# Two-block network on one core: the inverse's rank-1 updates on GpSimd instead of VectorE, a shorter round trip through DRAM sent by SyncE, and retention's table loaded with the other constants

## The chip, the cores and the metric

The kernel runs on one core of a Trainium2 chip. The metric is the device time of one execution in microseconds. A core has TensorE (PE, matrix products), VectorE (DVE), ScalarE (ACT), GpSimd (POOL) and SyncE (SP, which here only issues DMAs). Each engine works through its own list of instructions in the order of the program; an instruction that waits holds up everything behind it on its engine. The order is set when the kernel is built, by a scheduler that places instructions by priority and by its own estimate of when their inputs will be there; nothing is reordered while the kernel runs.

## The reference, cut to what matters

Two blocks of two layers each work on 256 tokens of width 1,024. Only the first block's two layers are touched. Each has a mixer with two branches, a gated delta rule and a retention:

```
lhs = jnp.eye(CHUNK) + a_mat                       # unit lower triangular
u = triangular_solve(lhs, vc * bc, ...)
w = triangular_solve(lhs, kb * exp(gc), ...)
...                                                # scan over chunks gives o
y_gdn  = (norm(o) * silu(gz)) @ w_br_gdn
scores = einsum(qc, kc) * dmask                    # retention, dmask = powers of a decay
y_ret  = (norm(retention) * silu(rg)) @ w_br_ret
merged = sigmoid(mg_ret) * y_ret + sigmoid(mg_gdn) * y_gdn
h = h + merged @ w_out
```

All weights and products are float32.

## The kernel before, in words

Every weight product is done in split float32: a block of weights (`raw`, 512 KB, six buffers, loaded by SP at L168) is copied by ACT to a rounded high part (`whi`, L247) and subtracted by DVE for the low part (`wlo`, L248), and TensorE then runs three matmuls (L195 to L197, or L221 to L223 for the transposed form) for each pair of tiles. One `raw` feeds 12 matmuls of 512 columns. There are three buffers of the pair `whi`, `wlo`. So the chain raw, whi, wlo, matmul runs all through the kernel, and the mixer's other work is put between its links.

In the mixer (`mixer1`, once per layer) `keys` makes the matrices `A` (8 heads by 2 chunks of 128, so 16 triangles of 128x128). Their inverses are needed by the delta rule. `small_blocks` inverts the 64 diagonal blocks of 32x32 of these 16 triangles: it sends the blocks of `A` through DRAM (`da`, L480, L486), so that one partition holds one block and half of its columns (`X`, named `na` in the code), starts from the unit matrix (`t`, tile `X2`), and applies 31 rank-1 updates, each a multiply into `w32` (L491) and a subtraction (L493). A transposed copy (`tt`, L494) is made, and both `t` and `tt` go back through DRAM (`dt`, L498, L499) into `tc32` (L501; shown as `tc` in the profile), with the blocks across partitions again. All these DMAs are issued by ACT. `invert` then builds `Tt` (L531) and `Tn` (L539) from `tc32` and joins the 32x32 blocks into 128x128 inverses, by small matmuls (L549 to L569) with a copy on ACT or a subtraction on DVE between each and the next; it is called for heads 0 to 3 (`i0`) and 4 to 7 (`i1`). `delta` (`d0`, `d1`) applies the delta rule to them (L585 to L633). `ORDER` names the sequence in which these and the gate and rotary projections are written; the scheduler interleaves them.

After that the retention runs in a pool of its own: two transposes per head (L696), a copy (`qkt`, L699, on ACT), scores (L701, L702), a multiplication by the table `ret` (`st`, L704, on DVE), and the output (L707 to L709), with the gates `mgg` and `mgr` (L640) between. The table is loaded in that pool (L690), whose memory becomes free when the delta rule's pool is done with it.

Of the kernel before, what the change touches and what calls it, by code (L numbers as in the profile page):

```python
# [9 lines left out]
F32 = mybir.dt.float32  # L10
# [5 lines left out]
P = 128  # L16
# [5 lines left out]
RAW2 = 6  # L22
CONV = 800
CRIT = 50
DQ = lambda nc: [nc.scalar]
ORDER = "z v0 v1 v2 v3 rg i0 d0+i1 d1 rq rk rv".split()
D = 1024
T = 256
# [50 lines left out]
    return {k: np.ascontiguousarray(v, dtype=f) for k, v in out.items()}  # L79


C1 = ("ident", "tri", "mask32", "eye32", "cos", "sin")
C2 = ("cum", "band", "bmask", "chunk")
CONST_W = {"ident": 128, "cos": 256, "sin": 256, "ret": 1536, "incl": 128, "tri": 256, "mask32": 128, "eye32": 512, "cum": 512,
           "band": 1536, "bmask": 256, "chunk": 2, "lt8": 64, "iota": 128}
# [20 lines left out]
class Net:  # L106
# [246 lines left out]
    def mixer1(s, h, l):  # L353
        nc, a = s.nc, s.a
# [3 lines left out]
        with ExitStack() as es:  # L358
            g1 = es.enter_context(s.tc.tile_pool(name="g1", bufs=1))
# [23 lines left out]
            g = g1.tile([P, 2, 8], F32, name="g")  # L383
# [5 lines left out]
            tri = s.c["tri"].rearrange("p (i d) -> p i d", i=2)  # L389
# [28 lines left out]
            ga = gc = None  # L418
# [48 lines left out]
            Am = A.rearrange("p h c d -> p (h c) d")  # L467
            tc32 = None

            def small_blocks():  # L470


                nonlocal tc32
                tc32 = gc.tile([P, 16, 2, 32], F32, name="tc32", bufs=1)
                da = s.dram.tile([4, 16, 32, 32], F32, name="da")
                dt = s.dram.tile([32, 4, 16, 2, 32], F32, name="dt")
                q = DQ(nc)
                for b in range(4):
                    r = slice(b * 32, b * 32 + 32)
                    q[b % len(q)].dma_start(da[b].rearrange("m j i -> j m i"), Am[r, :, r])  # L480
                na = gc.tile([P, 8, P], F32, name="X", bufs=1).rearrange("p a (b c) -> p (a b) c", c=32)
                t = gc.tile([P, 8, 64], F32, name="X2", bufs=1).rearrange("p a (b c) -> p (a b) c", c=16)
                tt = gc.tile([P, 16, 32], F32, name="tt", bufs=1)
                w = gc.tile([P, 144], F32, name="w32", bufs=1)
                for e in range(2):
                    q[0].dma_start(na[e * 64:e * 64 + 64], da.rearrange("b m j i -> (b m) j i"))  # L486
                nc.vector.tensor_copy(t, s.c["eye32"].rearrange("p (a b) -> p a b", a=32))
                for j in range(31):
                    n, m = 31 - j, j // 2 + 1
                    x = w[:, :n * m].rearrange("p (a b) -> p a b", a=n)  # L490
                    nc.vector.tensor_mul(x, na[:, j, j + 1:][:, :, None].to_broadcast([P, n, m]),  # L491
                                         t[:, j, :m][:, None, :].to_broadcast([P, n, m]))
                    nc.vector.tensor_sub(t[:, j + 1:, :m], t[:, j + 1:, :m], x)  # L493
                nc.vector.tensor_copy(tt, t.rearrange("p a b -> p b a"))  # L494

                for e in range(2):
                    at = slice(e * 64, e * 64 + 64)
                    q[0].dma_start(dt.rearrange("r b m i (e c) -> e i (b m) r c", e=2)[e, 0], t[at])  # L498
                    q[0].dma_start(dt.rearrange("(r e) b m i c -> e i (b m) r c", e=2)[e, 1], tt[at])  # L499
                for b in range(4):  # L500
                    q[0].dma_start(tc32[b * 32:b * 32 + 32].rearrange("p m i c -> p (m i c)"),  # L501
                                   dt[:, b].rearrange("r m i c -> r (m i c)"))

            vts = {}

# [17 lines left out]
            def invert(pr):  # L523

                Tt = gc.tile([P, 8, P], F32, name="Tt")
                Tn = gc.tile([P, 8, P], F32, name="Tn", bufs=1)
                X2 = gc.tile([P, 8, 64], F32, name="X2", bufs=1)
                inverse[pr] = Tt
                Av = Am[:, pr * 8:pr * 8 + 8]
                own = slice(pr * 8, pr * 8 + 8)  # L530
                nc.vector.tensor_mul(  # L531
                    Tt.rearrange("p a (b c) -> p a b c", b=4),
                    tc32[:, own, 1][:, :, None, :].to_broadcast([P, 8, 4, 32]),
                    s.c["mask32"].rearrange("p (b c) -> p b c", b=4)[:, None].to_broadcast([P, 8, 4, 32]))
                nc.gpsimd.memset(Tn[:32, :, 32:64], 0.0)

                for b in range(3):
                    r = slice(b * 32, b * 32 + 32)
                    nc.vector.tensor_copy(Tn[r, :, r].rearrange("p a (c e) -> p a e c", e=2),  # L539
                                          tc32[r, own, 0].rearrange("p a (e c) -> p a e c", e=2))  # L540
                yield

                blocks = [(slice(b, b + 32), slice(b + 32, b + 64)) for b in (0, 64)]
                at = lambda i: slice(i * 32, i * 32 + 32)
                eight = lambda x: x[:, :T].rearrange("p (a d) -> p a d", a=8)
                px = s.pb()
                for l, r in blocks:
                    for i in range(8):
                        nc.tensor.matmul(px[r, at(i)], Av[l, i, r], Tn[l, i, l], start=True, stop=True)  # L549
                    nc.scalar.activation(X2[r, :, :32], eight(px[r]), AF.Copy)  # L550
                py = s.pb()
                l, r = blocks[0]
                for i in range(8):
                    nc.tensor.matmul(py[r, at(i)], Tt[r, i, r], X2[r, i, :32], start=True, stop=True)
                nc.scalar.activation(Tn[r, :, l], eight(py[r]), AF.Copy, scale=-1.0)
                pt = s.pb()
                for l, r in blocks:
                    for i in range(8):
                        nc.tensor.matmul(pt[l, at(i)], X2[r, i, :32], Tt[r, i, r], start=True, stop=True)
                    nc.vector.tensor_sub(Tt[l, :, r], Tt[l, :, r], eight(pt[l]))  # L560
                yield

                px = s.pb()
                for i in range(8):
                    nc.tensor.matmul(px[64:, i * 64:(i + 1) * 64], Av[:64, i, 64:], Tn[:64, i, :64], start=True, stop=True)
                nc.scalar.activation(X2[64:].rearrange("p a d -> p (a d)"), px[64:], AF.Copy)
                pt = s.pb()
                for i in range(8):
                    nc.tensor.matmul(pt[:64, i * 64:(i + 1) * 64], X2[64:, i], Tt[64:, i, 64:], start=True, stop=True)  # L569
                nc.vector.tensor_sub(Tt[:64, :, 64:], Tt[:64, :, 64:], pt[:64].rearrange("p (a d) -> p a d", a=8))  # L570
                yield
# [86 lines left out]

            with ExitStack() as e2:
                ga = e2.enter_context(s.tc.tile_pool(name="ga", bufs=2))  # L660
                gm = ga.tile([P, 8, 2, P], F32, name="gm", bufs=1)
                nc.vector.tensor_mul(gm, tri[:, None, :1].to_broadcast([P, 8, 2, P]),
                                     g.rearrange("p c h -> p h c")[:, :, :, None].to_broadcast([P, 8, 2, P]))
                gh, gl = (ga.tile([P, 8, 2, P], F32R, name=n, bufs=1) for n in ("gh", "gl"))
                s.split(gh, gl, gm)
                after = ga.tile([P, P], F32R, name="after", bufs=1)
                nc.scalar.activation(after, tri[:, 1], AF.Copy)
                for gi in range(4):
                    keys(gi)
            with ExitStack() as e2:  # L670
                gc = e2.enter_context(s.tc.tile_pool(name="gc", bufs=2))
# [15 lines left out]
        with ExitStack() as es:  # L687
            g1 = es.enter_context(s.tc.tile_pool(name="r1", bufs=1))
            g2 = es.enter_context(s.tc.tile_pool(name="r2", bufs=2))
            tab = {"ret": s.cst("ret", g1)}  # L690
            mg, mg2 = (g1.tile([P, 2, D], F32, name=n) for n in ("mgr", "mgg"))
            for hd in range(4):
                p = s.pb()
# [21 lines left out]
                r = s.rsqrt(mv[:, :, 1], 2, 1.0, EPS)  # L715
# [571 lines left out]
    def run(s, out):  # L1287
# [53 lines left out]
        for l in range(2):  # L1341
            with ExitStack() as e2:
                cp = e2.enter_context(s.tc.tile_pool(name="cp1", bufs=1))
                s.c = {n: s.cst(n, cp) for n in C1[1:]}
                s.mixer1(h, l)
# [66 lines left out]
```

## Time and profile before

| | |
|---|---|
| median of three runs | 1975.84 us (1973.92 to 1982.09) |
| the profiled execution | 1979.73 us, span 1977.8 us |
| TensorE busy | 1926.8 us, 97% of the span |
| VectorE busy | 1460.8 us, 74% |
| ScalarE busy | 1190.0 us, 60% |
| GpSimd busy | 13.3 us, 1%, 29 instructions |
| DMA | 396.5 MB, 200 GB/s over the span |

Starts are in microseconds from the span's start. The first layer's mixer runs from the start to about 300 us, the second layer's from about 550 us to 880 us. "Busy" is the sum of an engine's instructions, overlaps counted once. The granted clock is 1.00 when TensorE runs at the upper of its two levels, 2.4 GHz, and 0.50 at the lower.

### The profile page before, as it was taken

The numbers are of one execution on the slowest core, as the hardware profiler recorded it, in microseconds if no ns is written. First come the engines' busy times: TensorE is split into PE (matmuls) and PEld (weight loads), VectorE is DVE, ScalarE is ACT, GpSimd is POOL, SyncE is SP. The second block draws the span as 40 slices with busy tenths as digits, with TensorE's granted clock in tenths as the row PEclk, the third lists the DMA queues.
The fourth block names the chain that finished last, engine by engine and source line by source line (L and its number), as shares of the span: only waits on it lengthen the run. The fifth ranks groups of instructions, "written<-read, shape, count | busy, mean of one in ns | idle before, by whom it ended". The sixth has DMA issues, their size and how long they took to land.

```text
span 1977.8 us, 30203 instructions
## 1 busy us (share of the span) xinstructions
PE 1926.8 (97%) x11194; PEld 1639.8 (83%) x11194; DVE 1460.8 (74%) x2623; ACT 1190.0 (60%) x1891; POOL 13.3 (1%) x29
## 2 busy tenths in 40 slices
PE   8999999999999999998999999999999999999997
PEld 7887777999888977787888888787769898879896
DVE  7987676665479885766998888888877565777564
ACT  7863445544478654455877777787755444566453
POOL 0000000000000000001000000000000000000000
PEclk9999999999999999999999999999999999999999
DMA  8567345555565564356798989995724555525552
GB/s 242 152 173 189 101 142 178 173 188 184 189 183 153 165 187 123 123 193 232 249 355 297 356 294 360 329 351 189 225 85 171 187 186 172 183 101 184 184 192 98
DMA packets 252845, 396.54 MB, mean 200 GB/s; under 512 B 31344, under 2 KB 107280, under 8 KB 252560
## 3 DMA queue, kind: packets, MB, share of 16 engines
q1 hardware_dynamic: 235056, 389.27, 60.2%
q10 hardware_dynamic: 17632, 5.24, 1.2%
q8 instruction: 90, 1.47, 0.3%
q14 instruction: 67, 0.55, 0.1%
HBM read 390.79 MB, written 3.67 MB: 199 GB/s over the span
## 4 chain that ended last, share of the span: by engine, by line
PE 85%; DVE 6%; ACT 3%; DMA 3%; issue 2%; ACTq 0%; SPq 0%; DVEq 0%
PE mm L196 18%; PE mm L197 18%; PE mm L195 17%; PE mm L239 5%; PE mm L241 5%; PE mm L240 5%; DVE wlo L248 3%; PE mm L222 2%; PE mm L223 2%; PE mm L221 2%; ACT whi L247 2%; PE pt L263 1%; PE pt L882 1%; PE pt L941 1%; DMA X<-da 1%
## 5 line engine op out<-in xcount | busy, mean ns | idle before, releaser
L248 DVE TENSOR_TENSOR wlo<-raw,whi 128x1024 fp32r<-128x1024 f32 (+3 forms) x748 | 878.1, 1184 | 356.4 <-ACT whi L247 345.0
L247 ACT ACTIVATE whi<-raw 128x1024 fp32r<-128x1024 f32 (+3 forms) x748 | 765.4, 1027 | 604.7 <-PE mm L197 375.5
L195 PE MATMUL mm<-whi,uh 128*128 128x512 f32 (+3 forms) x1312 | 503.5, 385 | 7.0 <-ACT whi L247 3.5
L196 PE MATMUL mm<-wlo,uh 128*128 128x512 f32 (+3 forms) x1312 | 505.1, 385 | 3.0 <-DVE wlo L248 2.5
L197 PE MATMUL mm<-whi,ul 128*128 128x512 f32 (+3 forms) x1312 | 500.5, 384 | 0.2
L196 PEld LDWEIGHTS mm<-wlo,uh 128*128 128x128 f32 x1312 | 248.8, 190 | 52.9 <-DVE wlo L248 11.7
L195 PEld LDWEIGHTS mm<-whi,uh 128*128 128x128 f32 x1312 | 248.6, 190 | 53.0 <-ACT whi L247 5.4
L197 PEld LDWEIGHTS mm<-whi,ul 128*128 128x128 f32 x1312 | 248.3, 190 | 42.4 <-DVE ul L251 1.1
L239 PE MATMUL mm<-uh,whi 128*128 128x256 f32 x864 | 242.3, 281 | 0.8 <-ACT uh L250 0.6
L241 PE MATMUL mm<-uh,wlo 128*128 128x256 f32 x864 | 242.0, 280 | 0.0
L240 PE MATMUL mm<-ul,whi 128*128 128x256 f32 x864 | 241.9, 280 | 0.0
L239 PEld LDWEIGHTS mm<-uh,whi 128*128 128x128 f32 x864 | 163.7, 189 | 1.9 <-ACT uh L250 1.1
L241 PEld LDWEIGHTS mm<-uh,wlo 128*128 128x128 f32 x864 | 163.8, 190 | 0.0
L240 PEld LDWEIGHTS mm<-ul,whi 128*128 128x128 f32 x864 | 162.2, 188 | 0.2
L197 PE MATMUL mm<-whi,hl 128*128 128x512 f32 x344 | 136.7, 397 | 0.0
L196 PE MATMUL mm<-wlo,hh 128*128 128x512 f32 x344 | 136.5, 397 | 0.0
L195 PE MATMUL mm<-whi,hh 128*128 128x512 f32 x344 | 136.2, 396 | 0.0
L223 PE MATMUL mm<-uh,wlo 128*128 128x256 f32 x384 | 108.8, 283 | 0.0
L221 PE MATMUL mm<-uh,whi 128*128 128x256 f32 x384 | 108.6, 283 | 0.0
L222 PE MATMUL mm<-ul,whi 128*128 128x256 f32 x384 | 108.5, 283 | 0.0
L250 ACT ACTIVATE uh<-pt,cols 128x256 fp32r<-128x256 f32 x152 | 64.8, 471 | 29.5 <-PE pt L882 9.0
L197 PEld LDWEIGHTS mm<-whi,hl 128*128 128x128 f32 x344 | 64.6, 188 | 15.9
(410 smaller groups left out, 2391.0 us busy)
## 6 DMA issues: line engine op xcount, KB each, us to landing
raw<-in_w_in_dram SPq DMA_DIRECT2D x176, 512.0 KB, 3.7
raw<-in_w_mlp_dram SPq DMA_DIRECT2D x128, 512.0 KB, 3.3
raw<-in_exp_w_down_dram SPq DMA_DIRECT2D x80, 512.0 KB, 5.8
raw<-in_exp_w_gate_dram SPq DMA_DIRECT2D x64, 512.0 KB, 5.7
raw<-in_exp_w_up_dram SPq DMA_DIRECT2D x64, 512.0 KB, 6.2
raw<-in_w_out_dram SPq DMA_DIRECT2D x32, 512.0 KB, 3.6
raw<-in_exp_w_gate_dram SPq DMA_DIRECT2D x32, 384.0 KB, 5.1
raw<-in_exp_w_up_dram SPq DMA_DIRECT2D x32, 384.0 KB, 4.3
```

The costliest lines, as they stand in the source:

```text
L195: nc.tensor.matmul(o, uh[:, u0 + k, tk], hi, start=first and k == 0, stop=False)
L196: nc.tensor.matmul(o, uh[:, u0 + k, tk], lo, start=False, stop=False)
L197: nc.tensor.matmul(o, ul[:, u0 + k, tk], hi, start=False, stop=last and k == kt - 1)
L221: nc.tensor.matmul(o[:, m], hi[:, k], uh[:, k, :], start=k == 0, stop=False)
L222: nc.tensor.matmul(o[:, m], hi[:, k], ul[:, k, :], start=False, stop=False)
L223: nc.tensor.matmul(o[:, m], lo[:, k], uh[:, k, :], start=False, stop=k == 7)
L239: nc.tensor.matmul(o[:, i], hi[:, k], uh[:, k, :], start=k == 0, stop=False)
L240: nc.tensor.matmul(o[:, i], hi[:, k], ul[:, k, :], start=False, stop=False)
L241: nc.tensor.matmul(o[:, i], lo[:, k], uh[:, k, :], start=False, stop=k == 7)
L247: nc.scalar.activation(hi, src, AF.Copy)
L248: nc.vector.tensor_sub(lo, src, hi.bitcast(F32))
L250: nc.scalar.activation(hi, src, AF.Copy, scale=col)
```

## The change

- `small_blocks`: the start copy, the 31 multiplies and subtractions and the copy to `tt` are GpSimd instructions now. Every DMA of the round trip is issued by SyncE. Only the transposed blocks `tt` are sent back (two `dt` writes instead of four, four reads of half the size), and VectorE turns them back with one transpose of 32x32 blocks. `tt` uses the memory of the delta rule's `S`, `tc32` that of `X`.
- `ret` is one of the constants that are loaded at the start of each layer.
- The decay matrix `gm` of the mixer's first part is made and split in four pieces instead of one, in a quarter of the memory.

```diff
-DQ = lambda nc: [nc.scalar]
...
-C1 = ("ident", "tri", "mask32", "eye32", "cos", "sin")
+C1 = ("ident", "tri", "mask32", "eye32", "cos", "sin", "ret")
...
-                tc32 = gc.tile([P, 16, 2, 32], F32, name="tc32", bufs=1)
-                dt = s.dram.tile([32, 4, 16, 2, 32], F32, name="dt")
-                q = DQ(nc)
+                dt = s.dram.tile([32, 4, 16, 32], F32, name="dt")
                 for b in range(4):
                     r = slice(b * 32, b * 32 + 32)
-                    q[b % len(q)].dma_start(da[b].rearrange("m j i -> j m i"), Am[r, :, r])
+                    nc.sync.dma_start(da[b].rearrange("m j i -> j m i"), Am[r, :, r])
...
-                tt = gc.tile([P, 16, 32], F32, name="tt", bufs=1)
+                tt = gc.tile([P, 4, P], F32, name="S", bufs=1).rearrange("p a (b c) -> p (a b) c", c=32)
...
-                    q[0].dma_start(na[e * 64:e * 64 + 64], da.rearrange("b m j i -> (b m) j i"))
-                nc.vector.tensor_copy(t, s.c["eye32"].rearrange("p (a b) -> p a b", a=32))
+                    nc.sync.dma_start(na[e * 64:e * 64 + 64], da.rearrange("b m j i -> (b m) j i"))
+                nc.gpsimd.tensor_copy(t, s.c["eye32"].rearrange("p (a b) -> p a b", a=32))
                 for j in range(31):
                     n, m = 31 - j, j // 2 + 1
                     x = w[:, :n * m].rearrange("p (a b) -> p a b", a=n)
-                    nc.vector.tensor_mul(x, na[:, j, j + 1:][:, :, None].to_broadcast([P, n, m]),
+                    nc.gpsimd.tensor_mul(x, na[:, j, j + 1:][:, :, None].to_broadcast([P, n, m]),
                                          t[:, j, :m][:, None, :].to_broadcast([P, n, m]))
-                    nc.vector.tensor_sub(t[:, j + 1:, :m], t[:, j + 1:, :m], x)
-                nc.vector.tensor_copy(tt, t.rearrange("p a b -> p b a"))
+                    nc.gpsimd.tensor_sub(t[:, j + 1:, :m], t[:, j + 1:, :m], x)
+                nc.gpsimd.tensor_copy(tt, t.rearrange("p a b -> p b a"))
                 for e in range(2):
-                    at = slice(e * 64, e * 64 + 64)
-                    q[0].dma_start(dt.rearrange("r b m i (e c) -> e i (b m) r c", e=2)[e, 0], t[at])
-                    q[0].dma_start(dt.rearrange("(r e) b m i c -> e i (b m) r c", e=2)[e, 1], tt[at])
+                    nc.sync.dma_start(dt.rearrange("(r e) b m c -> e r (b m) c", e=2)[e].rearrange("r q c -> q r c"),
+                                      tt[e * 64:e * 64 + 64])
+                tc32 = gc.tile([P, 8, P], F32, name="X", bufs=1).rearrange("p a (b c) -> p (a b) c", c=32)
+                tc32 = tc32.rearrange("p (i m) c -> p i m c", i=2)
                 for b in range(4):
-                    q[0].dma_start(tc32[b * 32:b * 32 + 32].rearrange("p m i c -> p (m i c)"),
-                                   dt[:, b].rearrange("r m i c -> r (m i c)"))
+                    nc.sync.dma_start(tc32[b * 32:b * 32 + 32, 1].rearrange("p m c -> p (m c)"),
+                                      dt[:, b].rearrange("r m c -> r (m c)"))
+                nc.vector.transpose(tc32[:, 0].rearrange("p m c -> p (m c)"), tc32[:, 1].rearrange("p m c -> p (m c)"))
...
-                gm = ga.tile([P, 8, 2, P], F32, name="gm", bufs=1)
-                nc.vector.tensor_mul(gm, tri[:, None, :1].to_broadcast([P, 8, 2, P]),
-                                     g.rearrange("p c h -> p h c")[:, :, :, None].to_broadcast([P, 8, 2, P]))
-                s.split(gh, gl, gm)
+                for i in range(4):
+                    hs = slice(i * 2, i * 2 + 2)
+                    gm = ga.tile([P, 2, 2, P], F32, name="gm", bufs=1)
...
+                    s.split(gh[:, hs], gl[:, hs], gm)
...
-            tab = {"ret": s.cst("ret", g1)}
+            tab = s.c
```

`invert` reads `tc32` in its new layout and is otherwise as before.

In the changed kernel every line has a number one to four lower (L491 is L488, L501 is L499 and the transpose is a new L501, L549 is L546, L699 is L698). The order that the scheduler made changes too, most of all in three places.

The first place is SP's list in the first layer, from the end of `keys` to the inverse. Before, nothing but loads of `raw` stands there. Now it reads so (X<-da fills `na`, X<-dt fills `tc32`):

```order
L477 DMA da<-A 32x16x32 x2
L167 DMA raw<-in_w_in_dram 128x2x512
L477 DMA da<-A 32x16x32
L167 DMA raw<-in_w_in_dram 128x2x512 x2
L477 DMA da<-A 32x16x32
L167 DMA raw<-in_w_in_dram 128x2x512
L483 DMA X<-da 64x1024
L167 DMA raw<-in_w_in_dram 128x2x512
L483 DMA X<-da 64x1024
L167 DMA raw<-in_w_in_dram 128x2x512 x6
L494 DMA dt<-S 64x16x32
...
L499 DMA X<-dt 32x512 x2
```

The round trip's ten later DMAs, from ACT's list before, stand among the loads of weights, which are behind them in the same list. The first dt<-S waits for GpSimd's last copy; six loads of `raw` stand between it and X<-da, and all that TensorE does ahead of the inverse uses `raw` loads that stand ahead of that dt<-S.

The second place is TensorE's list where `i0` begins. Before, in the first layer (the 32x32 matmuls are `invert`'s; L549 reads `Tn`):

```order
L195 MATMUL mm<-whi,uh 128x512
L549 MATMUL pt<-Tn,A 32x32 x8
L196 MATMUL mm<-wlo,uh 128x512
L197 MATMUL mm<-whi,ul 128x512
L195 MATMUL mm<-whi,uh 128x512
```

After, from the second group of eight of the same matmuls on:

```order
L546 MATMUL pt<-Tn,A 32x32 x8
L551 MATMUL pt<-X_1945,Tt 32x32 x8
L556 MATMUL pt<-Tt,X_1945 32x32 x8
L194 MATMUL mm<-whi,uh 128x512
L562 MATMUL pt<-Tn,A 64x64 x8
L195 MATMUL mm<-wlo,uh 128x512
L196 MATMUL mm<-whi,ul 128x512
L556 MATMUL pt<-Tt,X_1945 32x32 x8
```

The inverse stands earlier: between the last matmul that makes `A` and the first of `i0` there are 193 matmuls of 512 columns instead of 269 (in either layer), 76 fewer. Within `i0` and the delta rule, from the first L549 to the last L616, there are 81 instead of 97. Between the last L616 and retention's first L701 there are 29 instead of 18.

The third place is DVE's list there, after the change. The transpose waits for the four X<-dt, and the `wlo` behind it wait with it:

```order
L654 TENSOR_TENSOR qr<-qr,rtmp 128x512
L247 TENSOR_TENSOR wlo<-raw,whi 128x1024
L501 STREAM_TRANSPOSE X<-X 128x512
L530 TENSOR_TENSOR Tt<-X,c_mask_95 128x1024
L247 TENSOR_TENSOR wlo<-raw,whi 128x1024
L537 COPY Tn<-X 32x8x32 x3
```

Before, the 62 instructions of L491 and L493 stood in this list between `wlo`, conv and rotary instructions, and are gone from it. On GpSimd each of them waits for the one before, and nothing else stands between them.

## Rows read from the trace of the kernel before

**Rows 1.** Stretches (us): time, then busy us of PE, PEld, DVE, ACT, POOL; clock, DMA.

```profile
116.00:190.00 74.00, 70.00 (x334) 56.27 (x332) 57.23 (x127) 35.33 (x51) 0.30 (x1) 1.00 0.72 191
190.00:239.00 49.00, 47.99 (x431) 39.23 (x432) 30.31 (x61) 19.09 (x46) 0.46 (x1) 1.00 0.43 124
239.00:254.00 15.00, 11.80 (x50) 9.31 (x49) 8.12 (x28) 8.65 (x17) 0.00 (x0) 0.89 0.38 122
678.00:752.00 74.00, 70.01 (x334) 56.39 (x332) 57.20 (x127) 35.35 (x51) 0.30 (x1) 1.00 0.72 191
752.00:800.00 48.00, 47.73 (x429) 38.93 (x429) 30.13 (x61) 19.14 (x47) 0.46 (x1) 1.00 0.43 125
800.00:817.00 17.00, 13.83 (x58) 11.04 (x57) 9.09 (x29) 8.80 (x18) 0.00 (x0) 0.80 0.34 110
```

**Rows 2.** Waits of TensorE, 116 to 190 us: total us, times, longest.

```profile
PE pt L516 <- ACT cs L411: 1.7, 1, 1.7
PE mm L195 <- ACT whi L247: 1.3, 1, 1.3
```

**Rows 3.** Timeline, first layer, round trip: start, duration, engine, line [idle before].

```profile
116.15 0.37 ACTq L480 DMA_DIRECT2D da<-A  x1
...
135.47 0.19 DVE L491 TENSOR_TENSOR w<-X,X 128x31 f32<-128x31 f32 x1 [2.96 <-DMA X<-da]
...
177.30 0.61 DVE L494 COPY tt<-X 128x512 f32<-128x512 f32 x1
...
189.98 0.28 PE L549 MATMUL pt<-Tn,A 32*32 32x32 f32 x3 [0.47 <-DVE Tn L539]
```

**Rows 4.** Timeline, retention's start in the first layer, TensorE.

```profile
238.31 0.38 PE L616 MATMUL pt<-vn,qk 128*128 128x128 f32 x1
...
246.16 0.48 PE L701 MATMUL pt<-qkt 128*128 128x256 f32 x1 [2.12 <-ACT qkt L699]
```

**Rows 5.** Timeline, TensorE, two matmuls of 512 columns in sequence.

```profile
187.06 0.39 PE L196 MATMUL mm<-wlo,uh 128*128 128x512 f32 x1
187.29 0.39 PE L197 MATMUL mm<-whi,ul 128*128 128x512 f32 x1
```

**Rows 6.** Timeline, SyncE's issues of raw loads, first layer.

```profile
124.11 3.19 SPq L168 DMA_DIRECT2D raw<-in_w_in_dram  x2
```

**Rows 7.** DMA issues by tile: times, KB each, median us to landing.

```profile
c_ret<-in_c_ret_dram SPq DMA_DIRECT2D x2, 768.0 KB, 5.4
...
X<-da ACTq DMA_DIRECT2D x4, 256.0 KB, 6.9
tc<-dt ACTq DMA_DIRECT2D x8, 128.0 KB, 5.1
...
dt<-tt ACTq DMA_DIRECT2D x4, 128.0 KB, 4.8
```

**Rows 8.** The tile dt: how long an issue takes on its engine (ns min/median/max).

```profile
L499 ACTq DMA_DIRECT2D dt<-tt x4: 963/1326/1712, 177.9 to 744.2; - x4
```

**Rows 9.** GpSimd's instructions by line: busy us, mean ns of one.

```profile
L799 POOL TENSOR_TENSOR ul<-h,uh 128x512 fp32r<-128x512 f32 x4 | 5.1, 1282 | 28.7 <-ACT uh L798 28.7
...
L399 POOL MEMSET ci<- 128x6 f32 x2 | 0.2, 108 | 348.7 <-PE mm L197 348.4 <-POOLq L1402 0.3
```

**Rows 10.** Timeline, 927.5 to 928.7 us: ScalarE, VectorE and GpSimd.

```profile
927.87 0.62 ACT L798 ACTIVATE uh<-h 128x512 fp32r<-128x512 f32 x1
...
928.41 0.28 DVE L818 TENSOR_TENSOR gt<-lg 128x128 f32<-128x128 f32 x1
928.57 1.27 POOL L799 TENSOR_TENSOR ul<-h,uh 128x512 fp32r<-128x512 f32 x1 [1.93 <-ACT uh L798]
928.62 1.37 DVE L819 TENSOR_TENSOR eq<-eq,c_lt 128x128 f32<-128x128 f32 x1
```

**Rows 11.** VectorE, line 491: ns min/median/max, first and last start.

```profile
L491 DVE TENSOR_TENSOR w<-X,X x62: 163/259/301, 135.5 to 737.5; 128x126 f32<-128x126 f32 x6, 128x30 f32<-128x30 f32 x4, 128x56 f32<-128x56 f32 x4, 128x78 f32<-128x78 f32 x4
```

**Rows 12.** VectorE's groups by form, 140 to 180 us: busy us, mean ns.

```profile
L248 DVE TENSOR_TENSOR wlo<-raw,whi 128x1024 fp32r<-128x1024 f32 x14 | 17.1, 1221 | 0.0
```

More of the change, by code (lines that the diff above doesn't have):

```diff
@@ L532, in invert @@
                     Tt.rearrange("p a (b c) -> p a b c", b=4),
-                    tc32[:, own, 1][:, :, None, :].to_broadcast([P, 8, 4, 32]),
+                    tc32[:, 1, own][:, :, None, :].to_broadcast([P, 8, 4, 32]),
                     s.c["mask32"].rearrange("p (b c) -> p b c", b=4)[:, None].to_broadcast([P, 8, 4, 32]))
@@ L538, in invert @@
                     r = slice(b * 32, b * 32 + 32)
-                    nc.vector.tensor_copy(Tn[r, :, r].rearrange("p a (c e) -> p a e c", e=2),
-                                          tc32[r, own, 0].rearrange("p a (e c) -> p a e c", e=2))
+                    nc.vector.tensor_copy(Tn[r, :, r], tc32[r, 0, own])
                 yield
@@ L660, in mixer1 @@
                 ga = e2.enter_context(s.tc.tile_pool(name="ga", bufs=2))
-                gm = ga.tile([P, 8, 2, P], F32, name="gm", bufs=1)
-                nc.vector.tensor_mul(gm, tri[:, None, :1].to_broadcast([P, 8, 2, P]),
-                                     g.rearrange("p c h -> p h c")[:, :, :, None].to_broadcast([P, 8, 2, P]))
                 gh, gl = (ga.tile([P, 8, 2, P], F32R, name=n, bufs=1) for n in ("gh", "gl"))
-                s.split(gh, gl, gm)
+                for i in range(4):
+                    hs = slice(i * 2, i * 2 + 2)
+                    gm = ga.tile([P, 2, 2, P], F32, name="gm", bufs=1)
+                    nc.vector.tensor_mul(gm, tri[:, None, :1].to_broadcast([P, 2, 2, P]),
+                                         g.rearrange("p c h -> p h c")[:, hs, :, None].to_broadcast([P, 2, 2, P]))
+                    s.split(gh[:, hs], gl[:, hs], gm)
                 after = ga.tile([P, P], F32R, name="after", bufs=1)
```

## The prediction, made before the changed kernel ran

> **What bounds the kernel now.** I read the stretches first [rows 1]. Between the matrix `A` and the inverse TensorE works 70.00 us of 74, in the inverse and delta rule 47.99 of 49, at full clock. TensorE bounds the kernel, so time is won or lost only where TensorE idles or runs at its lower level. Two places have something to win. One is the round trip: 4.00 + 1.01 us idle in the first layer, 3.99 + 0.27 in the second, 9.27 in all. The named waits there are TensorE's on a ScalarE copy and on a `whi` [rows 2]; ScalarE issues the round trip's DMAs in that stretch, up to 1.7 us each [rows 8], and VectorE stands 2.96 us for X<-da [rows 3]. The other is retention's start: 3.20 and 3.17 us idle, 6.37, at a mean clock of 0.89 over 15 us and 0.80 over 17, which loses 15 x 0.11 = 1.65 and 17 x 0.20 = 3.4 us of full-clock time. That is 11.4 us at most. The longest single wait there is 2.12 us, the first L701 for `qkt` [rows 4].
>
> All removable loss together is about 20.7 us. One per cent is 19.8, so the change can win at most about that, and it moves a chain of 62 dependent instructions to another engine.
>
> **What it removes.** ScalarE issues none of these DMAs any more, and VectorE no longer stands at X<-da. I book the whole of the round trip's idle time: **-9.3**. (If the causes are others than I name, less.)
>
> VectorE also loses 62 instructions of about 0.26 us [rows 11] and a copy of 0.61, some 17 us per layer. It is busy 56.27 of 74 us there [rows 1], and TensorE hardly waits for it: 0.
>
> Retention: `qkt` waits for the tail of the delta rule on VectorE, and the table's load is not what TensorE waits for; the wait that goes is the 2.12 us. After the change 29 matmuls instead of 18 lie between the last L616 and the first L701. At 0.23 us each [rows 5], 11 more are 2.5 us, more than the wait. So at least 2 x 2.12 = 4.2 is won; with the rest of the idle time and the clock, at most 11.4. I take **-10**, near the upper end, because the low clock comes with the same gap.
>
> At nothing: `gm` in four pieces (same elements, VectorE and ScalarE idle enough in that stretch), and the earlier table, one more load of 5.4 us [rows 7] on SyncE, where six buffers of `raw`, each good for 12 x 0.23 = 2.76 us of TensorE, cover up to 16.6. Without that cover it would cost up to 5.4 per layer.
>
> **What it adds: a wait at the inverse.** The inverse now stands 76 matmuls earlier in TensorE's list. Before, its first matmul (L549) started at 189.98 [rows 3]. Without the 4.00 idle and the 76 x 0.23 = 17.5 us of matmuls, TensorE would now reach it at 168.5. The second layer has the same stretch, 678 to 752, with the same idle time, so the same holds there.
>
> When can the inputs be there? I follow the chain.
> - Start. The first da leaves at 116.15 as before. The later ones stand on SyncE among raw loads, whose issues last up to 3.19 us for two [rows 6]; the last da goes out at about 124.5 (estimate: where the third raw load stood before) and, at the 5.1 of tc<-dt [rows 7], has landed at 129.6. The second X<-da goes out behind one more raw load, about 130.4, and lands 6.9 later [rows 7]: 137. Before, it was 135.4 [rows 3].
> - GpSimd's 62 instructions: T, below.
> - After them: the copy to `tt`, on GpSimd between 0.61 [rows 3] and 1.28 [rows 9], I take 0.9; two dt<-S issues of 1.33 each, the median [rows 8], and landing 4.8 [rows 7]: with a short issue between, about 7.5; the last of the four X<-dt goes out some 2 us behind the first, 9.7 behind `tt`, and lands 5.1 later: 14.8. Then on VectorE the transpose (no row; 128x512 elements as in `tt`'s copy, 0.6), the multiply to `Tt` and the `wlo` between, 1.22 each [rows 12], and the first `Tn`, 0.3: **18**. Before, this tail took 189.98 - 177.30 = 12.7 with more waiting behind ScalarE and less behind SyncE.
>
> So the inverse can start at 137 + 18 + T = 155 + T, and TensorE stands for S = T - 13.5 us, if that is positive.
>
> **T.** No row shows a small two-input instruction on GpSimd. From what there is [rows 9]: 6 elements per partition take 108 ns and 512 take 1282 ns, so an element costs 1174 / 506 = 2.32 ns. The 31 steps have 2856 elements in all, 92 in the mean: 0.108 + 92 x 0.00232 = 0.32 us. The hand-over from one engine's end to GpSimd's start is 928.57 - 927.87 - 0.62 = 0.08 [rows 10]. That is 0.40 per instruction and **24.9 us** for 62, if nothing disturbs it.
>
> Something does. In [rows 10] VectorE's L819 with two inputs takes 1.37 us where L818 of the same size took 0.28, and it ends 0.15 behind the GpSimd instruction that began 0.05 ahead of it. VectorE stood still while GpSimd read. If that holds the other way round too, GpSimd stands still while VectorE makes a `wlo`, which has two inputs and takes 1.22. A `wlo` comes for every 12 matmuls, 2.76 us. Conv and rotary instructions, with two inputs also, come on top. In some 30 us eleven `wlo` fall, 11 x 1.22 = 13.4: **T = 38.3**. I take this, since `wlo` can't be done without and nothing in the program keeps the two apart. From below, T can't be expected under VectorE's own speed, 62 x 0.26 = 16.1. From above, 0.6 per instruction (half of the 1.28 of the 512-element row, [rows 9]) with the blocking gives 62 x 0.6 + 13.4 = 50.6.
>
> The Trainium skill (SBUF — State Buffer, section Who interferes with whom) says that such a VectorE instruction and a GpSimd instruction that reads SBUF contend, and that whichever starts first holds the shared ports to its end while the other fully blocks. The trace agrees in one direction, 1.37 against 0.28 us; the other, GpSimd behind a `wlo`, no run here shows. By the rule the sum is the one I take, without it the one of the first rival.
>
> With T = 38.3, S = 24.8 us per layer. After a stall of that length TensorE probably starts at its lower level, as at retention's start, where that lost 1.65 and 3.4; I take 2. Within the inverse and the delta rule 16 fewer matmuls (97 to 81, 3.7 us) lie between the links of the chain TensorE, ScalarE, TensorE, and three hand-overs have 0 or 1 between: between 0 and 3.7, I take 2.5.
>
> **Sum.** 2 x (24.8 + 2 + 2.5) - 9.3 - 10 = 58.6 - 19.3 = **+39.3**. Against the profiled execution, 1979.73 us (its span is 1977.8), that is 2019.0. It lies 3.89 above the median 1975.84, so the median after should be about **2015**.
>
> **Rivals.**
> 1. GpSimd isn't held up by VectorE (VectorE pays, with `wlo` standing behind short GpSimd instructions). T = 24.9, S = 11.4: 2 x 15.9 - 19.3 = +12.5, about **1988**. For it: the only overlap in the trace shows VectorE as the one that waits. Against it: sixty-two short instructions with a gap after each let VectorE in first again and again.
> 2. GpSimd's small broadcast instructions are slower than the line through two rows. T = 50.6, S = 37.1: 2 x 41.6 - 19.3 = +63.9, about **2040**. For it: these read strided and broadcast operands, the rows are plain ones.
> 3. Not slower: the chain is ready when TensorE comes. The sum is 2 x (S + 4.5) - 19.3, zero at S = 5.15, T = 18.7, which is 0.30 us for an instruction and its hand-over. At VectorE's speed, 16.1, S = 2.6: -5, and near -9 if the lower clock doesn't follow so short a stall, about **1967**. With no stall at all and the delta rule's cover still thinner, 5 - 19.3 = -14.3, 1961.5. For it: the inverse was put this early by a plan that counted on a short chain; the engine is otherwise free, 13.3 us busy in all. Against it: 0.30 would be less than the 0.40 that the two rows give with no disturbance.
>
> A fourth way, that raw loads behind the waiting dt<-S starve TensorE, changes nothing: what TensorE does ahead of the inverse uses loads that stand before it, and the six buffers refill while the inverse's small matmuls run.
>
> **How the numbers follow.** Likeliest, with blocking: 0.46. No blocking: 0.26. Slower instructions with blocking: 0.13. Not slower: 0.15. This kernel's measurement can tell about 0.5%, 9.9 us, from no change; the sum 2 x (T - 13.5 + 4.5) - 19.3 stays within that for T from 13.7 to 23.6. From the last case 0.07 is faster and 0.08 the same, and from the no-blocking case, which lies just above the bound, 0.11 is the same: faster 0.07, same 0.19, slower 0.74. The range cuts about a tenth on either side: 1972 (the last case's faster half) to 2042 (slow instructions). The likeliest case alone, eight to fourteen `wlo` in the chain: T 34.7 to 42, 2008 to 2023.
>
> **What the profile after would show.** On GpSimd, 62 instructions per layer at L488 and L490, of 0.3 us alone and longer beside a `wlo`; the time from the first L488 to `tt` is T. TensorE idle 20 to 30 us ahead of L546, released by VectorE's `Tn`, with the granted clock at half behind it; `wlo` waiting behind the transpose (L501); SyncE's list standing at dt<-S for GpSimd. The idle time in the stretch before is gone, and L700 waits no longer for `qkt`. I would be wrong if T is near 20 us, or if the inverse is reached later than 168.5 because something else holds TensorE ahead of it; and by tens of us too low if single instructions there take 0.6 or more.

## The result, and the profile after

The changed kernel takes 2021.95 us (median of four runs, 2018.54 to 2025.19), the kernel before 1974.88 on the same chip: a ratio of 1.0236, with a 95% interval of 1.0217 to 1.0255. The profiled executions differ by 2020.4 - 1977.8 = 42.6 us of span, where the prediction's sum was 39.3.

TensorE's waits of the whole changed kernel come first (total us, times, longest). One wait of 25 us in each layer has taken the place of all that stood there before [rows 2], and retention's wait of 2.12 us [rows 4] has shrunk to 0.3:

```profile
PE pt L546 <- DVE Tn L537: 49.8, 2, 25.3
...
PE pt L700 <- ACT qkt L698: 0.6, 2, 0.3
```

The stretches that answer to [rows 1] (us; time, then busy us of PE, PEld, DVE, ACT, POOL; clock, DMA) are those from the end of `keys` to TensorE's arrival at the inverse, the wait, the inverse with the delta rule, and retention's start:

```profile
116.00:168.40 52.40, 52.40 (x257) 42.49 (x256) 33.93 (x46) 28.21 (x44) 26.39 (x44) 1.00 0.54 136
168.40:193.70 25.30, 0.02 (x2) 0.01 (x1) 3.17 (x5) 2.11 (x2) 7.34 (x21) 0.59 0.51 145
193.70:241.00 47.30, 47.24 (x392) 39.01 (x393) 27.91 (x61) 14.56 (x34) 0.30 (x1) 0.82 0.30 79
241.00:258.00 17.00, 16.72 (x88) 13.59 (x87) 12.81 (x35) 8.37 (x24) 0.00 (x0) 1.00 0.47 124
```

TensorE has no idle time left ahead of the inverse (52.40 of 52.40) and hardly any at retention (16.72 of 17, at full clock). In between it stands 25.3 us, and the inverse behind it runs at a mean clock of 0.82, where it was 1.00.

The timeline of the first layer's round trip answers to [rows 3] (start, duration, engine, line; in brackets the idle time before and what ended it):

```profile
132.16 0.48 SPq L483 DMA_DIRECT2D X<-da  x1
...
139.16 1.32 POOL L488 TENSOR_TENSOR w<-X,X 128x31 f32<-128x31 f32 x1 [22.76 <-DMA X<-da]
...
141.56 0.28 POOL L488 TENSOR_TENSOR w<-X,X 128x58 f32<-128x58 f32 x1
141.85 1.23 DVE L247 TENSOR_TENSOR wlo<-raw,whi 128x1024 fp32r<-128x1024 f32 x1 [1.47 <-ACT whi L246]
141.93 1.32 POOL L490 TENSOR_TENSOR X<-X,w 128x58 f32<-128x58 f32 x1
...
143.33 0.28 POOL L488 TENSOR_TENSOR w<-X,X 128x56 f32<-128x56 f32 x1
...
168.02 0.39 PE L194 MATMUL mm<-whi,uh 128*128 128x512 f32 x1
...
176.30 1.03 POOL L491 COPY S<-X 128x512 f32<-128x512 f32 x1
177.35 0.66 SPq L494 DMA_DIRECT2D dt<-S  x1
...
190.50 0.71 DVE L501 STREAM_TRANSPOSE X<-X 128x512 f32<-128x512 f32 x1 [24.88 <-DMA X<-dt]
...
193.69 1.06 PE L546 MATMUL pt<-Tn,A 32*32 32x32 f32 x16 [25.28 <-DVE Tn L537]
...
243.71 1.16 PE L613 MATMUL pt<-vn,qk 128*128 128x128 f32 x8
```

Four things are to be read here. `X` arrives at 139.16 instead of 135.47. Among instructions of 0.28 us, one of the same size takes 1.32: it began 0.08 us behind a `wlo` on VectorE and ended 0.17 us behind that one's end. TensorE is done with everything ahead of the inverse at 168.4, while GpSimd's chain runs to 176.2. From the end of the copy it is 16.4 us more until the inverse starts, in DMAs and on VectorE. The last line is the end of the delta rule.

The granted clock behind the wait, in stretches of the same columns:

```profile
195.00:205.00 10.00, 10.00 (x90) 7.63 (x90) 3.75 (x8) 1.57 (x4) 0.30 (x1) 0.50 0.34 103
205.00:210.00 5.00, 5.00 (x24) 3.75 (x24) 4.31 (x7) 1.06 (x1) 0.00 (x0) 0.50 0.16 14
210.00:215.00 5.00, 5.00 (x31) 4.36 (x30) 2.23 (x4) 1.33 (x2) 0.00 (x0) 0.96 0.24 91
```

TensorE is busy all the time from 195 us on, and is granted its lower level for 15 us and more after the wait is over.

### The profile page after: what moved, and what is told of

Same layout as the page of the kernel before. It is cut to its first block, busy times and chain, and to the rows that moved or that the text cites. A ratio compares the mean times of both kernels' runs of the same rounds, so it can differ in the third digit from the quotient of the medians.

```text
span 2020.4 us, 30224 instructions
## 1 busy us (share of the span) xinstructions
PE 1934.1 (96%) x11194; PEld 1648.3 (82%) x11194; DVE 1443.0 (71%) x2509; ACT 1192.5 (59%) x1897; POOL 80.6 (4%) x157
## 4 chain that ended last, share of the span: by engine, by line
PE 83%; DVE 6%; POOL 3%; ACT 3%; DMA 2%; issue 2%; SPq 0%; ACTq 0%; DVEq 0%; POOLq 0%
PE mm L195 18%; PE mm L196 17%; PE mm L194 17%; PE mm L238 5%; PE mm L240 5%; PE mm L239 5%; DVE wlo L247 3%; ACT whi L246 2%; POOL w L488 2%; POOL X L490 2%; PE mm L222 1%; PE mm L221 1%; PE mm L220 1%; PE pt L262 1%; PE pt L881 1%
```

## The experiments

The theory is that of the prediction: GpSimd's chain, drawn out by VectorE's `wlo`, is far longer than the time that TensorE takes to reach the inverse in the new order, and the wait lies on TensorE's path. Against it stand three others: SyncE sends the round trip too late; GpSimd's instructions are simply slow; the order of the rest, not the chain, makes the loss.

**The chain on VectorE again, the rest of the change kept.**

```diff
-                nc.gpsimd.tensor_copy(t, ...)
+                nc.vector.tensor_copy(t, ...)
...
-                    nc.gpsimd.tensor_mul(x, ...)
+                    nc.vector.tensor_mul(x, ...)
```

(and so for the subtraction and the copy to `tt`).

> The changed kernel with the start copy, the 62 instructions and the copy to tt back on VectorE; the DMAs on SyncE, the single transposed write and the early table stay. 301 instead of 193 of the counted matmuls stand ahead of the inverse, 70 in it, 13 ahead of retention's scores. My theory (GpSimd's chain is longer than the place of the inverse allows): TensorE waits under 6 us per layer for the inverse, retention's wait of 2 to 3 us is back, 1965 to 1985 us. Rival (the round trip is late because SyncE sends it between loads of weights): a wait of 15 us or more per layer stays, 2000 us or more.

Measured 1970.59 us, a ratio of 0.9963 (0.9945 to 0.9981): slightly faster than before. Two lines of VectorE's chain, and the only wait of over 1 us in the first layer's mixer:

```profile
137.68 0.19 DVE L488 TENSOR_TENSOR w<-X,X 128x31 f32<-128x31 f32 x1 [0.34 <-DMA X<-da]
...
172.99 0.60 DVE L491 COPY S<-X 128x512 f32<-128x512 f32 x1
```

```profile
PE pt L700 <- ACT qkt L698: 4.1, 1, 4.1
```

The wait for the inverse is gone and retention's is back, as expected (4.1 us, not 2 to 3). Mixed with `wlo` and rotary work on VectorE, the chain is 35 us long, hardly shorter than GpSimd's 37. But here the scheduler placed the inverse behind 301 matmuls instead of 193, and 108 matmuls are 24.8 us of TensorE's time, about the wait itself. So this run shows that the later place takes the wait away, not that SyncE's sending costs nothing. What that costs can be bounded from the timelines: of the 25.3 us, 3.7 come from the later `X`, and 4.3 from the way back, which took 16.4 us from the copy's end where it took 189.98 - 177.91 = 12.1 before. SyncE's sending is at most these 8 us of the wait, not the greater part of it.

**Nothing but the chain on GpSimd.** The kernel before, with the start copy, the 62 instructions and the copy to `tt` on GpSimd (the diff above the other way round).

> The kernel before with nothing but the start copy, the 62 instructions and the copy to tt on GpSimd; DMAs on ScalarE, both writes, late table. 157 matmuls stand ahead of the inverse, 34 ahead of retention's scores. My theory: GpSimd's chain of about 38 us alone makes the loss; TensorE idles 20 to 30 us per layer, part of it now for whi, since ScalarE's list stands at dt<-X; 2005 to 2030 us. Rival (SyncE's sending is the cost): under 1985 us.

Measured 2001.67 us, 1.0111 (1.0082 to 1.014): slower, but less than expected (2005). TensorE's longest wait, GpSimd's first instruction and copy, and ScalarE's first `whi` behind the DMA that waits for GpSimd:

```profile
PE mm L195 <- ACT whi L247: 16.5, 1, 16.5
```

```profile
134.69 0.24 POOL L491 TENSOR_TENSOR w<-X,X 128x31 f32<-128x31 f32 x1 [17.02 <-DMA X<-da]
...
166.26 1.04 POOL L494 COPY tt<-X 128x512 f32<-128x512 f32 x1
...
166.99 1.06 ACT L247 ACTIVATE whi<-raw 128x1024 fp32r<-128x1024 f32 x1 [22.46 <-POOL X L493]
```

ScalarE's list stands at the DMA that waits for GpSimd, `whi` stands behind it, and TensorE waits for `whi` instead of the inverse. With no `whi` there is no `wlo` either, so GpSimd's chain took only 166.26 - 134.69 = 31.6 us, which I had not seen coming: the wait shortens the chain that causes it. So the chain on GpSimd alone, in the order that the scheduler makes for it, makes the kernel slower, with none of SyncE's sending.

**No `wlo` on VectorE beside the chain.** The subtraction is left out while the delta rule's pool is open; `lo` is a copy of `raw` there, made by ScalarE.

```diff
-            nc.vector.tensor_sub(lo, src, hi.bitcast(F32))
+            if getattr(s, "alone", False):
+                nc.scalar.activation(lo, src, AF.Copy)
+            else:
+                nc.vector.tensor_sub(lo, src, hi.bitcast(F32))
```

> The changed kernel, but in the stretch of the delta rule's pool wlo is a copy of raw made by ScalarE, which leaves out the subtraction of whi there, so that VectorE runs no wlo beside GpSimd's chain. The inverse stands at the same place counted in full matmuls. My theory (GpSimd stands still while VectorE makes a wlo): GpSimd's 62 instructions take 25 to 29 us instead of 37.1, none over 0.8 us but beside rotary, TensorE's wait for the inverse falls from 25 to 13 to 17 us per layer, 1995 to 2008 us. Rival (the instructions are just that slow, or wait for something else): the chain stays at 35 us or more, 2015 to 2028 us.

Measured 1998.04 us, 1.0096 (1.0066 to 1.0125), as the theory said. Lines of GpSimd's timeline there, one of VectorE's, and TensorE's wait:

```profile
143.81 0.24 POOL L491 TENSOR_TENSOR w<-X,X 128x31 f32<-128x31 f32 x1 [21.06 <-DMA X<-da]
...
152.00 0.40 POOL L491 TENSOR_TENSOR w<-X,X 128x126 f32<-128x126 f32 x1
...
159.83 0.78 DVE L657 TENSOR_TENSOR qr<-qr,rtmp 128x512 f32<-128x512 f32 x1
...
160.14 0.74 POOL L491 TENSOR_TENSOR w<-X,X 128x130 f32<-128x130 f32 x1
...
172.26 1.05 POOL L494 COPY S<-X 128x512 f32<-128x512 f32 x1
```

```profile
PE pt L549 <- DVE Tn L540: 14.7, 1, 14.7
```

The 62 instructions take 172.2 - 143.8 = 28.4 us instead of 37.1. The few long ones left stand beside rotary's sums, which have two inputs in SBUF (0.74 beside L657). Beside rotary's products, which read one input from PSUM, none does. The rival that the instructions are just that slow is out: nine of the 37 us are VectorE's. The wait fell by 10.5 us, more than the 8.7 of the chain, since the place wasn't the same as I had expected: TensorE's list has 23 more matmuls between `A` and the inverse (216 against 193), `X` comes 4.7 us later, and from `X` to TensorE's arrival at the inverse it is 31.0 us instead of 29.3.

**The inverse held back, GpSimd's chain kept.** Its first matmuls on TensorE, the transpose on VectorE and the way back on SyncE are queued behind the last projection (`at_pe`, `at_dve` and `at_sp` are the last instruction of a projection, of rotary and of a load on these engines).

```diff
-ORDER = "z v0 v1 v2 v3 rg i0 d0+i1 d1 rq rk rv".split()
+ORDER = "z v0 v1 v2 v3 rg rq rk rv b i0 d0+i1 d1".split()
...
+                with s.tc.issue_after(s.at_sp.ins), s.tc.issue_after(s.at_dve.ins):
...
+                behind = s.tc.issue_after(s.at_pe.ins) if not pr else nullcontext()
```

> The changed kernel with GpSimd's chain as it is, but the inverse is written behind all of rotary's and the gates' projections, and its first matmuls on TensorE, the transpose on VectorE and the way back on SyncE are queued behind the last of these. 288 instead of 193 of the counted matmuls stand ahead of the inverse, 18 instead of 29 ahead of retention's scores. My theory (the loss is GpSimd's chain against the place of the inverse): TensorE comes 95 x 0.23 = 22 us later, some four more wlo fall in the chain, the wait falls from 25 to 5 to 12 us per layer, 1980 to 1996 us. Rival (GpSimd's instructions beside VectorE's cost what they cost, wherever the inverse stands): 2010 us or more.

Measured 2001.64 us, 1.0126 (1.011 to 1.0143): 20 us better than the change, but not the 26 to 42 expected. The way back in the first layer:

```profile
183.85 0.66 SPq L497 DMA_DIRECT2D dt<-S  x1
...
200.19 0.71 DVE L504 STREAM_TRANSPOSE X<-X 128x512 f32<-128x512 f32 x1 [14.85 <-DMA X<-dt]
...
204.53 1.06 PE L552 MATMUL pt<-Tn,A 32*32 32x32 f32 x16 [13.30 <-DVE Tn L541]
```

The wait fell from 25 to 13.3 and 11.6 us, where 5 to 12 were expected. The chain grew as I had worked out (the copy ends 44 us behind the first instruction, with `wlo` beside it to its end), but the way back also grew, from 16.4 to 20.7 us, and retention's wait of 2.1 us came back because 18 matmuls were left ahead of it. Place and chain both count, and a later place lengthens the chain. The round trip counts too: the inverse starts 14.5 us later than in the kernel before (189.98), behind a chain hardly longer than VectorE's there (42.9 us against 41.8); `X` came 4.3 us later and the way back took 8.6 longer.

**Half of the chain.**

```diff
-                for j in range(31):
+                for j in range(0, 31, 2):
```

> The changed kernel with every second of the 31 rank-1 steps left out, so that the inverse's small blocks are not those of the reference; 32 instead of 62 instructions per layer on GpSimd. The inverse stands 11 full matmuls earlier (2.5 us). My theory (the wait follows the chain's length one for one): the chain is about 19 instead of 37 us, the wait falls from 25 to 8 to 11 us per layer, 1980 to 1995 us. Rival (the wait is mostly the DMAs around the chain): over 18 us per layer, 2005 us or more.

Measured 2002.34 us, 1.0127 (1.0111 to 1.0144): above what I expected. The end of the chain, ScalarE's and VectorE's lists, and TensorE's three longest waits in the first layer:

```profile
161.97 1.08 POOL L491 COPY S<-X 128x512 f32<-128x512 f32 x1
...
168.18 1.06 ACT L246 ACTIVATE whi<-raw 128x1024 fp32r<-128x1024 f32 x1 [8.59 <-DMA raw<-in_w_in_dram]
...
177.62 0.71 DVE L501 STREAM_TRANSPOSE X<-X 128x512 f32<-128x512 f32 x1 [15.03 <-DMA raw<-in_w_in_dram]
178.25 1.18 DVE L247 TENSOR_TENSOR wlo<-raw,whi 128x1024 fp32r<-128x1024 f32 x1
```

```profile
PE mm L195 <- DVE wlo L247: 9.5, 1, 9.5
PE mm L194 <- ACT whi L246: 2.6, 1, 2.6
PE pt L546 <- DVE Tn L537: 1.8, 1, 1.8
```

In the inverse behind them:

```profile
182.00:200.00 18.00, 17.96 (x133) 13.91 (x133) 9.42 (x16) 2.77 (x5) 0.30 (x1) 0.50 0.36 100
```

The wait is 14 us instead of 8 to 11, and its name has changed: loads of `raw` stand behind dt<-S, and a `wlo` behind the transpose, so TensorE lacks `wlo` rather than `Tn`. Half the instructions took 21.5 us, not 19, because `wlo` ran beside them to the end. The wait still follows the chain's end, though not one for one: the chain ends 14.3 us earlier (161.9 instead of 176.2), and the inverse starts 11.7 us earlier (182.0 instead of 193.7), since the way back from the copy's end took 19.0 us instead of 16.4. So it isn't mostly the DMAs. The time fell by 20 us instead of the 27 or more expected: the wait is longer than expected, and the granted clock behind it is 0.50 for as long as in the changed kernel (18 us and 16.7).

**Only the early table.** The kernel before with the table among the constants, `gm` in four pieces and the memory this needs.

```diff
-C1 = ("ident", "tri", "mask32", "eye32", "cos", "sin")
+C1 = ("ident", "tri", "mask32", "eye32", "cos", "sin", "ret")
...
-            tab = {"ret": s.cst("ret", g1)}
+            tab = s.c
```

> The kernel before with the table loaded with the constants and gm in four pieces (and tt and tc32 in the memory of S and X, to make room); rank-1 updates on VectorE, DMAs on ScalarE, both writes. 26 instead of 18 matmuls stand ahead of retention's first score. My theory of that term (8.4 us won in the changed kernel, by more matmuls ahead of L700): the wait for qkt falls from 2.12 to about 0.3 us, the clock stays up there, 1964 to 1972 us. Rival (the early table wins nothing by itself): 1972 to 1980 us.

Measured 1996.32 us, 1.0082 (1.0055 to 1.011). Both of my answers were wrong: it is some 18 us slower than the kernel before (1978.20 on the same chip). TensorE's waits in the first layer's inverse, one of ScalarE's issues, and the stretch of the inverse:

```profile
PE pt L550 <- DVE Tn L540: 3.4, 2, 1.8
PE pt L555 <- DVE Tt L532: 2.0, 1, 2.0
```

```profile
183.95 3.18 ACTq L498 DMA_DIRECT2D dt<-S  x1
```

```profile
190.00:215.00 25.00, 19.51 (x149) 14.57 (x148) 9.70 (x15) 8.04 (x12) 0.46 (x1) 0.74 0.44 127
```

The table moved the whole order: 77 matmuls instead of 97 stand between the links of the inverse, and ScalarE issues DMAs (3.18 us for one) where `whi` is needed. TensorE idles 5.5 us in 25 and drops to its lower level. Retention's wait is 1.6 us, with 26 matmuls ahead of it, where I expected 0.3.

**The same with SyncE sending** (`DQ = lambda nc: [nc.sync]`).

> The kernel with only the early table (chain on VectorE, both writes), its DMAs on SyncE instead of ScalarE. 300 instead of 281 of the counted matmuls stand ahead of the inverse, 0 instead of 26 ahead of retention's first score. My theory (that kernel was 20 us slower because ScalarE's issues of up to 3.2 us hold whi, and with it TensorE, so that its clock falls): no wait of over 1 us for Tn, Tt or whi, the clock stays at 1.00 in the inverse; retention's wait for qkt is longer, 4 to 8 us; 1970 to 1986 us. Rival (the early table or gm in pieces costs by itself): the waits for Tn and Tt stay, 1990 us or more.

Measured 1991.58 us, 1.0062 (1.0045 to 1.0079). Retention's wait and two stretches:

```profile
PE pt L704 <- ACT qkt L702: 5.3, 1, 5.3
```

```profile
190.00:215.00 25.00, 24.31 (x193) 19.22 (x192) 13.61 (x18) 9.68 (x12) 0.46 (x1) 1.00 0.66 177
...
239.00:262.00 23.00, 17.02 (x82) 14.60 (x82) 12.87 (x52) 7.71 (x24) 0.00 (x0) 0.77 0.00 0
```

The waits in the inverse went, as expected of ScalarE's issues (24.31 of 25 us at full clock). But no filling matmul was left ahead of retention, and 6 us of idle time with a clock of 0.77 appeared there. The total of 1991.58 lies above my range and in the rival's, though not for the rival's reason: no wait for `Tn`, `Tt` or `whi` of over 1 us is left, and the loss moved. What early table and `gm` cost by themselves can't be told apart from the order they bring.

**Retention's wait.** In the trace of the kernel before, `qkt` (L699) itself waits for L629, the last reader of the small factors `rq8`, in both layers (us, times):

```profile
  DVE rs_y L629: 0.8, 2
```

It takes over their memory.

```diff
-            bk, ik, rq8 = (g1.tile([P, 2, 8], F32, name=n) for n in ("bk", "ik", "rq8"))
+            bk, ik = (g1.tile([P, 2, 8], F32, name=n) for n in ("bk", "ik"))
+            rq8 = m8.tile([P, 2, 8], F32, name="rq8")
```

> The kernel before with one thing moved: the small factors rq8 (64 bytes per partition) lie in the mixer's lasting pool m8 instead of g1, whose memory retention's qkt takes over. My theory of retention's wait (qkt waits for L629 because it takes the place of rq8, which L629 reads last): L701 waits under 0.6 us instead of 2.12 and the clock stays up there, 1963 to 1971 us. Rival (qkt waits for the delta rule's end anyway, or ScalarE is late): L701 still waits about 2 us, within 0.3% of before.

Measured 1967.42 us, 0.9955 (0.9939 to 0.9972). The two stretches of [rows 1] are now full, at full clock:

```profile
239.00:254.00 15.00, 15.00 (x77) 12.10 (x76) 11.60 (x37) 9.40 (x22) 0.00 (x0) 1.00 0.46 146
800.00:817.00 17.00, 17.00 (x85) 13.81 (x84) 15.93 (x64) 8.14 (x15) 0.00 (x0) 1.00 0.44 130
```

20 matmuls stand ahead of the first score there, 18 before, which is too little to cover the wait. So 64 bytes of memory per partition, not the table, held retention.

**The fastest combinations.** The chain on VectorE with SyncE sending the one write, and `rq8` in `m8`; then the same with the table late and `gm` whole.

> The changed kernel with its chain on VectorE and rq8 in m8. 24 instead of 13 matmuls stand ahead of retention's first score. My theory: no wait at the inverse and the 4.1 us wait at L700 mostly gone with its low clock, 1948 to 1962 us, the fastest so far. Rival (another wait takes the place of that at L700, or the inverse has too few matmuls in it): as with the chain on VectorE alone, 1963 to 1975 us.

> The fastest kernel so far (chain on VectorE, one transposed write by SyncE, rq8 in m8), with the table loaded in retention's own pool and gm in one piece, as before. The counted matmuls stand as they stood. My theory (the early table wins nothing): 1954 to 1963 us, no new wait at retention. Rival (the early table is part of the gain): st waits for the table, 1966 us or more.

Measured 1958.8 us, 0.9906 (0.989 to 0.9923), and 1956.15 us, 0.9892 (0.9865 to 0.992): both faster than either kernel. The intervals overlap, so no gain of the early table shows. What difference there is lies in the first one's first layer, where the granted clock fell with no idle time ahead of it:

```profile
198.40:208.60 10.20, 10.20 (x52) 7.85 (x50) 3.24 (x6) 1.65 (x2) 0.20 (x1) 0.50 0.25 74
```

From the inverse to the delta rule's end that layer takes 45.9 us, where its second layer and both of the other kernel take 41.4. The second kernel's stretches in the first layer show no idle time at all:

```profile
116.00:190.00 74.00, 74.00 (x353) 60.74 (x352) 62.01 (x129) 39.45 (x56) 0.01 (x1) 1.00 0.78 207
190.00:215.00 25.00, 25.00 (x278) 20.22 (x277) 14.45 (x24) 8.82 (x14) 0.30 (x1) 1.00 0.39 107
215.00:239.00 24.00, 24.00 (x171) 20.52 (x169) 14.84 (x39) 12.16 (x41) 0.00 (x0) 1.00 0.37 101
239.00:262.00 23.00, 23.00 (x113) 18.84 (x112) 21.98 (x97) 10.31 (x14) 0.00 (x0) 1.00 0.43 135
```

## Why the prediction was right, and where its terms were off

- **Arrival.** TensorE reached the inverse at 168.41 (forecast 168.5): the 9.27 us of idle time went as booked, and the 76 matmuls were worth what their row said.
- **Start.** `X` came at 139.16, not 137. SyncE's issues of loads between the DMAs took longer than taken, up to 3.5 us for two, and the second X<-da left at 132.16 instead of 130.4.
- **T.** 176.23 - 139.16 = 37.1 us against 38.3, by two errors that nearly cancel, so that the small miss is luck. Undisturbed instructions are slower than the line through two rows made them: 28.4 us for all 62 with no `wlo` beside (a few still behind rotary) instead of 24.9. And the blocking cost some 9 us instead of 13.4. In the changed kernel's first layer ten of the 62 take over 1.1 us, each beside a `wlo`; with VectorE's list standing at the transpose from 165.6 us on, no `wlo` ran beside the chain's last ten us.
- **The lock, the other way round.** What the prediction only inferred is shown by the 1.32 beside 0.28 us and by the run without `wlo`. The rule of the Trainium skill (SBUF — State Buffer, section Who interferes with whom), that whichever starts first keeps the shared ports and the other fully blocks, agrees with the trace in this direction also (1.32 us behind a `wlo` that began 0.08 us earlier). Of the ten long ones, one began 0.01 us ahead of its `wlo` and was still the one held up.
- **The way back.** 17.4 us with the copy, forecast 18. The prediction's own terms add up to 18 without the copy's 0.9, so with it the forecast should have been 19.
- **The wait.** 25.3 and 24.5 us, forecast 24.8.
- **The clock and the inverse's cover.** I took 2 + 2.5 us per layer. From the first matmul of the inverse to the last L613 it is 51.2 us where it was 49.5, with 16 matmuls fewer (3.7 us) and without 1.01 us of idle time: 6.4 us lost in the first layer (6.5 in the second). TensorE idles 0.06 us there, so the cover cost nothing, and what is left to explain it is the clock, which was granted at 0.50 for 16.7 us: the term of 2 was three times too small. In retention's rows, from which I took it, the lower level lasts 3.4 and 6.8 us, behind waits of 2.1; here it lasts 16.7, behind 25.
- **Retention.** Forecast -10. Idle time fell from 6.37 to about 0.6 us and the clock stayed at 1.00, where it had lost 1.65 + 3.4: some -11. The number was near, and the reason given (more matmuls ahead of L700) holds: over the kernels that leave `rq8` where it was, the wait is 5.3 us with 0 matmuls ahead, 4.1 with 13, 2.1 with 18, 1.6 with 26 and 0.3 with 29. But the cause of the wait was only half named: "the tail of the delta rule" is L629, by way of the memory of `rq8`, and the run with only the early table won nothing.
- Together: 2 x (24.9 + 6.4) - 9.3 - 11 = 42.3, against 42.6 between the spans.
- **What I set aside too easily** is that loads behind dt<-S can starve TensorE. In the changed kernel TensorE has no such wait (that its longer chain hides it is not shown); in the run with half of the chain they do, for 2.6 us and, with `wlo` behind the transpose, for 9.5 more.
- **What neither the prediction nor my theory said.** The chain isn't longer on GpSimd. Before, it took 41.8 us on VectorE ([rows 3], 135.47 to 177.30), and its copy ended at 177.9; now it takes 37.1 and the copy ends at 177.3. The wait comes from the other side: TensorE asks for the inverse 21.1 us earlier (168.4 instead of 189.5), and the way back is 4.3 longer. Two pairs of kernels differ in their text by the chain's engine alone, and in both the scheduler puts the inverse much earlier for GpSimd: behind 157 instead of 269 matmuls (the kernel before with the chain moved), and behind 193 instead of 301 (the changed kernel), some 25 us each, for a chain that ran 10 us shorter in one pair and 2 us longer in the other. The prediction's sum holds all the same, since it took the new place from the new order. Blocked instructions made the chain nine us longer than it need be. But by an estimate from these rows, the 76 matmuls in their old place would have filled 17.5 of the 25.3 us.

Not settled: how much of the other kernels' losses is the order that the scheduler makes of any edit, since most of them moved the inverse. No run kept the order word for word while only the engine changed, and why the scheduler asks for GpSimd's result so early stays open.

## What to carry to other kernels

Work on an idle engine isn't free when it is a long chain with a deadline: compare its end with the moment when the bottleneck asks for it in the new order, and let the plan know its true length (no run here did that). Compare it also with the length that the chain really had on the old engine, between that engine's other work: here 41.8 us, not the 16 of its instructions alone. Instructions with two inputs in SBUF on VectorE, and GpSimd's own, held each other up to the end of the one that began first (0.28 us became 1.32), so a chain of short ones next to long ones pays the long one's time again and again. Ahead of moving work, ask what a named wait really waits for: here 64 bytes per partition of reused memory cost 9 us.

## What I had not expected of the hardware

- TensorE's clock stays at its lower level long after the work is back: from the wait's end at 193.7 to 210.4 us it was granted 0.50, though it was busy all the time. In the kernel with only the early table it fell at 202.2 us, during the third of three waits of 1.7, 1.8 and 2.0 us within nine us. With the chain on VectorE and `rq8` moved it fell at 198.4 with no wait ahead of it, while the inverse's small matmuls ran.
- A blocked instruction ends shortly behind the other engine's, in both directions: GpSimd's 1.32 us ends 0.17 behind its `wlo` and the 0.74 ends 0.27 behind a rotary sum, and VectorE's 1.37 in [rows 10] ends 0.15 behind GpSimd's.
- GpSimd's short instructions with broadcast inputs take 0.40 us at 126 elements, and 62 of them take 28.4 us with little beside them, less than the 35 to 42 us that VectorE needs for the same chain between its other work.
